# Seven-product block multiplication for the recurrent branch's projections, with gate projections set between the heads

## Chip, core and metric

The kernel runs on one NeuronCore of a Trainium2 chip. The metric is the device time of one execution in microseconds (us), the median over several runs. TensorE does the matrix products, VectorE (DVE), ScalarE (ACT) and GpSimd (POOL) the elementwise work, and SyncE (SP) issues nearly all DMAs. Each engine works through its own list of instructions in order; the lists are fixed when the program is built.

## The reference

One layer of a hybrid model on x of 1024 tokens by 1024 features, float32 throughout. All streams come from one projection of x:

```
(a_q ... b_u, b_v, b_z, c_q, c_k, c_v, c_if, c_o, c_z, m_g) = split(x @ w_in)
y_a = nsa(...) * silu(a_z)                       # sparse attention
y_b = spatial_gating(b_u, b_v, ...) * silu(b_z)  # 128x128 mixing per chunk of tokens
y_c = mlstm(c_q, c_k, c_v, c_if, c_o, ...) * silu(c_z)
merged = sum over 3 branches of sigmoid(m_g[branch]) * (y_branch @ w_br[branch])
r = ALPHA * x + merged @ w_out
out = layernorm(r + sigmoid(r @ ple_gate) * (p @ ple_w))
```

The recurrent branch `mlstm` has 4 heads of 128 features. For each head it passes c_q and c_k through a causal convolution of 4 taps, a bias and a silu; it then runs over 8 chunks of 128 tokens, with a state matrix carried from chunk to chunk; the result is normalized and multiplied by sigmoid(c_o) and silu(c_z). m_g holds 3 x 1024 gate features.

## The kernel before

**Number format.** Every product with x or another wide operand is made from split operands: each float32 tile is cut into a high part `hi` (a cast to the type that TensorE reads faster, by ACT) and a remainder `lo` (a subtraction on DVE), and hi x hi, lo x hi and hi x lo are summed in PSUM. So one 128x128x512 block product is three matmuls. A plain projection of 128 features (`wf`, then `proj_half` on L129 twice) takes 8 blocks of the 1024 inputs, 3 matmuls each, for two halves of 512 tokens: 48 matmuls. `load_w` (L92, L93) loads and splits its weights.

**Strassen for the gates.** The 24 blocks of gate features are taken in 12 pairs. A pair is a product of a 2x2 block matrix of weights (two feature blocks, two halves of the inputs) with a 2x2 block matrix of x (two halves of the inputs, two halves of the tokens). `strassen` (L886) makes it with seven block products instead of eight: 7 x 4 x 3 = 84 matmuls (L907). For each product the left operand is a sum of weight blocks (`total`, DVE, L899), split into `sh` (ACT, L893) and `sl` (DVE, L894); partial results are kept by ACT (L912), added by DVE (L945), and put through tanh by ACT (L947). The right operands are x's own tiles or the sums `T1` to `T4`, made once before the first pair (L861 to L884): DVE or POOL subtractions, then `split_op` (L857, L858).

**Order of the work.** The program is written with tile pools; a tool puts the instructions into each engine's list by its own estimate of when each is ready, taking the one that is first in program order among those ready, and adds the waits. When a pool is closed and another opened in its place, a tile of the new pool waits for those tiles of the old one that lay at the same addresses. Tiles of one tag share that tag's buffers.

The stages are: attention (fillers: a_z, b_u, b_z projections); then pool `pq`: the token-side value projections `proj_tok256` (L150) for b_v and then c_v (into `V1`, L686); the spatial gating (8 chunks c: L706, mixing matmuls L710 with `wT`, 4 DVE operations L713 and 4 L716 per chunk, one buffer `mt`); the four heads; then `pq` closes, `pg` opens, T1 to T4 and the 12 gate pairs; then `pf`, the merge of the branches (L956 on).

A head before: `conv_proj` twice (wf, taps L739 and L742, tanh and L745), the chunk loop (L766 to L804), small statistics (L805 to L814), the c_z and c_o projections into `oz` (L816 to L833), and transposes, product `yc` and store to `ysc` (L834 to L843). Each head has 4 plain projections.

Of the kernel before, what the change touches and what calls it, by code (L numbers as in the profile page):

```python
# [45 lines left out]
def hybrid_kernel(ctx, tc, xm, pT, wfm, wvg, wtm, cmpw1, cmpw2, cpos, vecs, sgwT, sgb,  # L46
# [680 lines left out]
    def conv_proj(i, nm):  # L727
        w = wf(FM["cq"] + i)
        xq = pq.tile([P, T + 4], F32, tag="xpad", bufs=1, name="xpad")
        nc.gpsimd.memset(xq[:, 0:4], 0.0)  # L730
        for half in range(2):
            po = pj()
            proj_half(po, w, half, xh, xl)
            nc.scalar.copy(xq[:, 4 + half * 512:516 + half * 512], po)
        r = pq.tile([P, T], F32, tag=nm, bufs=1, name=nm)

        def tap(j):
            return vec[:, C_CW + 4 * i + j:C_CW + 4 * i + j + 1]
        vv.tensor_scalar(out=r, in0=xq[:, 4:4 + T], scalar1=tap(3), scalar2=vec[:, C_CB + i:C_CB + i + 1],  # L739
                         op0=OP.mult, op1=OP.add)  # L740
        for j in range(3):
            stt(out=r, in0=xq[:, 1 + j:1 + j + T], scalar=tap(j), in1=r, op0=OP.mult, op1=OP.add)  # L742
        t = pq.tile([P, T], F32, tag="cth", bufs=1, name="cth")
        act(t, r, AF.Tanh, scale=0.5)
        stt(out=r, in0=t, scalar=1.0, in1=r, op0=OP.add, op1=OP.mult)  # L745
        return r

    for h in range(NH_C):
        yc = pq.tile([P, T], F32, tag="yc", bufs=4, name="yc")
        k2 = conv_proj(4 + h, "k2")  # L750
# [1 line left out]
        eb = pq.tile([P, NT, P], F32, tag="eb", bufs=1, name="eb")
        ub = pq.tile([P, NT, P], F32, tag="ub", bufs=1, name="ub")
        nc.sync.dma_start(ub.rearrange("p c t -> p (c t)"), uscr[0, h:h + 1, :].to_broadcast([P, T]))
        nc.sync.dma_start(eb.rearrange("p c t -> p (c t)"), uscr[1, h:h + 1, :].to_broadcast([P, T]))
        for c in range(NT):
            act(ub[:, c, :], ub[:, c, :], AF.Exp, bias=cols[:, 0, 8 * h + c:8 * h + c + 1], scale=-1.0)
        nc.gpsimd.affine_select(out=ub, in_=ub, pattern=[[0, NT], [1, P]], compare_op=OP.is_ge,
                                fill=0.0, base=0, channel_multiplier=-1)
        qe = pq.tile([P, T], F32, tag="qe", bufs=1, name="qe")  # L760
        for c in range(4):
            s = slice(c * 256, c * 256 + 256)
            nc.gpsimd.tensor_mul(qe[:, s], q2[:, s], eb.rearrange("p c t -> p (c t)")[:, s])
        nb = pq.tile([P, NT, 129], F32, tag="nb", bufs=1, name="nb")
        mv = pq.tile([P, NT, 2], F32, tag="mv", bufs=1, name="mv")
        C1 = None  # L766

        def intra(c):
            s = slice(c * P, c * P + P)
            psS = pst("st", 2, "ps_cs")  # L770
            mm(psS[:, 0:P], lhsT=k2[:, s], rhs=q2[:, s], start=True, stop=True)
            Wt = pq.tile([P, P], F32, tag="Wt", bufs=2, name="Wt")
            stt(out=Wt, in0=psS[:, 0:P], scalar=CS, in1=ub[:, c, :], op0=OP.mult, op1=OP.mult)
            ke = None
            if c < NT - 1:
                pk = pst("m", 2, "ps_k")
                nc.tensor.transpose(pk[:, 0:P], k2[:, s], ident)
                ke = pq.tile([P, P], F32, tag="ke", bufs=2, name="ke")
                nc.scalar.mul(ke, pk[:, 0:P], cols[:, 2, 8 * h + c:8 * h + c + 1])
            return Wt, ke  # L780

        nxt = intra(0)
        for c in range(NT):
            s = slice(c * P, c * P + P)
            Wt, ke = nxt
            if c < NT - 1:
                nxt = intra(c + 1)
            pn = pst("o", 2, "ps_n")
            mm(pn[:, 0:129], lhsT=Wt, rhs=V1[:, c, h, :], start=True, stop=(c == 0))
            if c > 0:  # L790
                mm(pn[:, 0:129], lhsT=qe[:, s], rhs=C1, start=False, stop=True)
            nc.scalar.copy(nb[:, c, :], pn[:, 0:129])
            s6 = pq.tile([P, 6], F32, tag="s6", bufs=2, name="s6")
            vv.bn_stats(out=s6, in_=nb[:, c, 0:P])
            vv.bn_aggr(out=mv[:, c, :], in_=s6)
            if c < NT - 1:
                pu = pst("m", 2, "ps_u")
                mm(pu[:, 0:129], lhsT=ke, rhs=V1[:, c, h, :], start=True, stop=True)
                Cn = pq.tile([P, 129], F32, tag="C1", bufs=2, name="C1")
                if C1 is None:  # L800
                    vv.tensor_copy(Cn, pu[:, 0:129])
                else:
                    stt(out=Cn, in0=C1, scalar=eb[:, c, P - 1:P], in1=pu[:, 0:129], op0=OP.mult, op1=OP.add)
                C1 = Cn  # L804
        dn = pq.tile([P, NT], F32, tag="dn", bufs=1, name="dn")  # L805
        stt(out=dn.unsqueeze(2), in0=nb[:, :, P:P + 1], scalar=-1.0, in1=nb[:, :, P:P + 1], op0=OP.mult, op1=OP.max)
        vv.tensor_max(dn, dn, cols[:, 1, 8 * h:8 * h + 8])
        vv.reciprocal(dn, dn)
        ve = pq.tile([P, NT], F32, tag="ve", bufs=1, name="ve")
        vv.tensor_mul(ve, mv[:, :, 1], dn)  # L810
        vv.tensor_mul(ve, ve, dn)
        vv.tensor_scalar_add(ve, ve, EPS)
        rs = rsqrt_small(pq, ve, [P, NT], "rsc")
        vv.tensor_mul(rs, rs, dn)  # L814

        oz = pq.tile([P, T], F32, tag="oz", bufs=1, name="oz")  # L816
        w = wf(FM["cz"] + h)
        for half in range(2):
            po = pj()
            proj_half(po, w, half, xh, xl)  # L820
            s = slice(half * 512, half * 512 + 512)
            act(oz[:, s], po, AF.Tanh, scale=0.5)
            stt(out=oz[:, s], in0=oz[:, s], scalar=1.0, in1=po, op0=OP.add, op1=OP.mult)
        w = wf(FM["co"] + h)
        for half in range(2):
            po = pj()
            proj_half(po, w, half, xh, xl)
            s = slice(half * 512, half * 512 + 512)
            t = tp.tile([P, 512], F32, tag="ge_a", bufs=2, name="oth")
            act(t, po, AF.Tanh, scale=0.5)  # L830
            stt(out=oz[:, s], in0=t, scalar=1.0, in1=oz[:, s], op0=OP.add, op1=OP.mult)
        vv.tensor_scalar(out=oz, in0=oz, scalar1=vec[:, C_NG + h:C_NG + h + 1], scalar2=0.25,
                         op0=OP.mult, op1=OP.mult)  # L833
        for hf in range(2):  # L834
            pt = pst("o", 2, "ps_h")
            for cc in range(4):
                c = 4 * hf + cc
# [371 lines left out]
```

## Time and profile before

| what | value |
|---|---|
| median of 3 runs | 1386.09 us (1385.65 to 1388.98) |
| profiled execution | 1386.04 us |
| its span, first to last instruction | 1384.3 us |
| mean granted TensorE clock | 0.994 of full |
| PE, PEld, DVE, ACT, POOL busy | 98%, 83%, 58%, 35%, 12% |

PE is TensorE's matmuls, PEld its weight loads, which run beside the matmuls. A matmul's bar in the profile is its duration; bars of neighbours overlap, so the time a matmul takes in a stream is read from one start to the next. L-numbers are lines of the kernel before. "x48" is a count. In a list of waits, "A <- B" says that A sat idle until B was done.

### The profile page before, as it was taken

The numbers are of one execution on the slowest core, as the hardware profiler recorded it, in microseconds if no ns is written. First come the engines' busy times: TensorE is split into PE (matmuls) and PEld (weight loads), VectorE is DVE, ScalarE is ACT, GpSimd is POOL, SyncE is SP. The second block draws the span as 40 slices with busy tenths as digits, with TensorE's granted clock in tenths as the row PEclk, the third lists the DMA queues.
The fourth block names the chain that finished last, engine by engine and source line by source line (L and its number), as shares of the span: only waits on it lengthen the run. The fifth ranks groups of instructions, "written<-read, shape, count | busy, mean of one in ns | idle before, by whom it ended". The sixth has DMA issues, their size and how long they took to land. (4 is left out here: it accounts for less than half of the span.)

```text
span 1384.3 us, 18935 instructions
## 1 busy us (share of the span) xinstructions
PE 1355.4 (98%) x7231; PEld 1148.0 (83%) x7231; DVE 804.4 (58%) x1882; ACT 484.9 (35%) x974; POOL 162.1 (12%) x179
## 2 busy tenths in 40 slices
PE   9999999999999999999999979999999999999997
PEld 7977888887888999988888868888888887888786
DVE  7236687536787636486755775544545545334855
ACT  6353424243343333122332354444442212223211
POOL 0011211101221110020100000000000344000312
PEclk9999999999999999999999989999999999999999
DMA  9131101111120032142113123232248543113211
GB/s 313 31 82 34 31 21 46 30 54 55 39 69 5 17 108 78 47 152 92 62 61 92 51 103 116 97 122 107 107 145 318 196 148 121 46 61 123 98 39 46
DMA packets 39420, 123.27 MB, mean 89 GB/s; under 512 B 4761, under 2 KB 7705, under 8 KB 39329
## 3 DMA queue, kind: packets, MB, share of 16 engines
q1 hardware_dynamic: 38368, 118.91, 25.1%
q0 software_dynamic: 960, 3.15, 1.0%
q8 instruction: 57, 0.93, 0.3%
q14 instruction: 35, 0.28, 0.1%
HBM read 98.91 MB, written 23.13 MB: 88 GB/s over the span
## 5 line engine op out<-in xcount | busy, mean ns | idle before, releaser
L129 PE MATMUL ps_pj<-xh,whi 128*128 128x512 f32 x544 | 217.3, 399 | 2.3 <-DVE QA L402 2.3
L129 PE MATMUL ps_pj<-xh,wlo 128*128 128x512 f32 x544 | 216.8, 399 | 0.0
L129 PE MATMUL ps_pj<-xl,whi 128*128 128x512 f32 x544 | 215.2, 396 | 0.0
L536 PEld LDWEIGHTS ps_o<-V,pt 128*128 128x128 f32 x912 | 117.5, 191 | 12.2 <-ACT pt L516 3.3
L129 PEld LDWEIGHTS ps_pj<-xh,whi 128*128 128x128 f32 x544 | 102.3, 188 | 22.8 <-PE ps_pj L129 3.9
L129 PEld LDWEIGHTS ps_pj<-xl,whi 128*128 128x128 f32 x544 | 102.4, 188 | 18.9
L129 PEld LDWEIGHTS ps_pj<-xh,wlo 128*128 128x128 f32 x544 | 102.7, 189 | 17.5
L536 PE MATMUL ps_o<-V,pt 128*128 128x65 f32 x912 | 116.6, 269 | 0.5 <-POOL pt L518 0.3
L92 ACT CAST whi<-wraw 128x1024 fp32r<-128x1024 f32 x62 | 65.0, 1048 | 106.8 <-PE ps_b L129 51.6
L516 ACT ACTIVATE pt<-ps_st 128x512 f32<-128x512 f32 x114 | 65.3, 594 | 103.9 <-PE ps_st L514 96.8
L93 DVE TENSOR_TENSOR wlo<-wraw,whi 128x1024 fp32r<-128x1024 f32 x62 | 81.2, 1310 | 20.5 <-ACT whi L92 20.3
L979 POOL TENSOR_TENSOR M<-M,gt 128x512 f32<-128x512 f32 x32 | 42.8, 1349 | 350.4 <-DVE gt L978 334.8
L129 PE MATMUL ps_b<-sp_hi,wlo 128*128 128x512 f32 x192 | 74.7, 389 | 0.0
L129 PE MATMUL ps_b<-sp_hi,whi 128*128 128x512 f32 x192 | 74.7, 389 | 0.0
L129 PE MATMUL ps_b<-sp_lo,whi 128*128 128x512 f32 x192 | 74.1, 390 | 0.0
L907 PE MATMUL ps_a<-op_hi,sh 128*128 128x512 f32 x144 | 56.0, 389 | 0.0
L907 PE MATMUL ps_a<-op_hi,sl 128*128 128x512 f32 x144 | 56.0, 389 | 0.0
L907 PE MATMUL ps_a<-op_lo,sh 128*128 128x512 f32 x144 | 56.0, 389 | 0.0
L894 DVE TENSOR_TENSOR sl<-ss,sh 128x512 fp32r<-128x512 f32 x48 | 33.1, 692 | 35.2 <-ACT sh L893 34.9
L1024 PE MATMUL ps_g<-gh,sp_hi 128*128 128x512 f32 (+1 forms) x144 | 52.7, 366 | 0.0
L1024 PE MATMUL ps_g<-gh,sp_lo 128*128 128x512 f32 (+1 forms) x144 | 52.7, 366 | 0.0
L1024 PE MATMUL ps_g<-gl,sp_hi 128*128 128x512 f32 (+1 forms) x144 | 52.6, 366 | 0.0
(360 smaller groups left out, 3117.7 us busy)
## 6 DMA issues: line engine op xcount, KB each, us to landing
wraw<-in_wfm_dram SPq DMA_DIRECT2D x34, 512.0 KB, 3.6
mraw<-in_wfm_dram SPq DMA_DIRECT2D x24, 512.0 KB, 3.6
gsc<-gt SPq DMA_DIRECT2D x24, 512.0 KB, 2.6
gt<-gsc SPq DMA_DIRECT2D x24, 512.0 KB, 6.0
xraw<-in_xm_dram SPq DMA_DIRECT2D x14, 512.0 KB, 6.8
wraw<-in_wbr_dram SPq DMA_DIRECT2D x12, 512.0 KB, 4.4
yraw<-ysc SPq DMA_DIRECT2D x12, 512.0 KB, 4.3
wraw<-in_wtm_dram SPq DMA_DIRECT2D x8, 512.0 KB, 3.8
```

Source lines behind the costliest of these rows:

```text
L92: nc.scalar.copy(hi[:, c], raw[:, c])
L93: vv.tensor_sub(lo[:, c], raw[:, c], hi[:, c])
L129: mm(po[:M, :], lhsT=a[:, k, :], rhs=b(k, half), start=(i == 0), stop=(i == n - 1))
L516: act(pt.rearrange("p h q -> p (h q)"), sp, AF.Exp)
L536: mm(po[:, h * 65:h * 65 + 65], lhsT=pt[:, h, :], rhs=V[:, j, vi, :], start=(first and h == 0), stop=last, skip_group_check=True)
L894: vv.tensor_sub(lo, src, hi)
L907: mm(bank, lhsT=l[a][:, k, :], rhs=r[b], start=first and k == 0 and i == 0, stop=k == K - 1 and i == 2, skip_group_check=True)
L979: nc.gpsimd.tensor_add(M[n][:, s], M[n][:, s], t[:, s])
L1024: mm(po[:, 0:n], lhsT=a[k][:, ts_], rhs=b[k][:, s], start=(k == 0 and i == 0), stop=(k == KT - 1 and i == 2))
```

## The change

- The eight plain projection pairs of the heads become Strassen pairs: c_k with c_q (`conv_pair`), c_z with c_o (`oz_pair`). All Strassen pairs share `strassen`; its product order becomes B11, T1, T2, B21, T3, B22, T4, its third bank comes from tag "st" instead of "o", and `sh`, `sl`, `ss` have 3 buffers instead of 4.
- T1 to T3 are made beside the b_v projections and T4 after the c_v projections, in a new pool `pt` that stays open below `pq` and `pg`.
- `pq` closes right after the spatial gating, and `pg` opens there. c_v is written to DRAM (`v1scr`) from small tiles `vs` and read back per head into a one-head `V1`.
- The 12 gate pairs are no longer one block: each head issues two of them (`mg_pair`), one between `conv_pair` and `oz_pair` and one after the head's chunks; four follow at the end. Their results `gt` use the weight tag "wlo" instead of "y".
- In the heads k2, q2, oz, eb, ub, qe, nb and the padded inputs take the shared tag "y" (8 buffers); the chunk's PSUM tiles move from "st" and "m" to "m" and "o". The first tap and the scaling of oz go from DVE to ACT; tanh of the convolution is made in halves.

```diff
+    right = {n: [None, None] for n in ("T1", "T2", "T3", "T4")}
+    t4 = []
+    for m in range(2):
+        b11, b12, b22, b21 = (yp.tile([P, T], F32, tag="y", bufs=YB, name="xraw") for _ in range(4))
+        for t, (mm_, j) in zip((b11, b12, b22, b21), ((m, 0), (m, 1), (m + 2, 1), (m + 2, 0))):
+            nc.sync.dma_start(t, xm[mm_, j])
+        vv.tensor_sub(b11, b12, b11)
+        right["T1"][m] = split_op(b11, pt_, "t", 12)
+        vv.tensor_sub(b12, b22, b12)
+        vv.tensor_sub(b22, b22, b11)
+        right["T2"][m] = split_op(b22, pt_, "t", 12)
+        right["T3"][m] = split_op(b12, pt_, "t", 12)
+        vv.tensor_sub(b21, b21, b22)
+        t4.append(b21)
...
-    V1 = pq.tile([P, NT, NH_C, 129], F32, name="V1")
+    v1scr = dr.tile([NH_C, P, NT, P], F32, name="v1scr")
     for wi in range(2):
         for i, po in enumerate(proj_tok256(wtm[2 + wi], xh, xl)):
...
+            vs = pq.tile([P, 2, 2, P], F32, tag="vs", bufs=2, name="vs")
+            nc.any.tensor_copy(out=vs.rearrange("p j a d -> p (j a d)"), in_=po)
+            for a in range(2):
+                nc.sync.dma_start(v1scr[2 * wi + a, :, 2 * i:2 * i + 2, :], vs[:, :, a, :])
+    for m in range(2):
+        right["T4"][m] = split_op(t4[m], xp, "x", 16)
...
+    pq_ctx.close()
+    pg_ctx = ExitStack()
+    pg_ = pg_ctx.enter_context(tc.tile_pool(name="pg", bufs=1))
+    pq = pg_
+    ng4 = pg_.tile([P, 4], F32, name="ng4")
...
+            hi = pg_.tile([P, 512], F32R, tag="sh", bufs=3, name="sh")[:, 0:w]
+            lo = pg_.tile([P, 512], F32R, tag="sl", bufs=3, name="sl")[:, 0:w]
...
+    def mg_pair(q):
+        gt = [wp.tile([P, T], F32, tag="wlo", bufs=WB, name="gt") for _ in range(2)]
...
+    def conv_pair(h):
...
+        strassen_fm(FM["ck"] + h, FM["cq"] + h, done)
...
+            act(r, x[:, 4:4 + T], AF.Identity, scale=tap(3), bias=vec[:, C_CB + i:C_CB + i + 1])
+            for j in range(3):
+                stt(out=r, in0=x[:, 1 + j:1 + j + T], scalar=tap(j), in1=r, op0=OP.mult, op1=OP.add)
+            for half in range(2):
...
+                stt(out=r[:, s], in0=t, scalar=1.0, in1=r[:, s], op0=OP.add, op1=OP.mult)
...
     for h in range(NH_C):
...
-        k2 = conv_proj(4 + h, "k2")
-        q2 = conv_proj(h, "q2")
+        k2, q2 = conv_pair(h)
+        mg_pair(2 * h)
+        oz = oz_pair(h)
+        V1 = pq.tile([P, NT, 129], F32, tag="V1", bufs=1, name="V1")
+        nc.gpsimd.memset(V1[:, :, 128:129], 1.0)
+        nc.sync.dma_start(V1[:, :, 0:P], v1scr[h])
...
+        nc.sync.dma_start(ysc[2][h], oz)
+        mg_pair(2 * h + 1)
+    for q in range(8, 12):
+        mg_pair(q)
     pg_ctx.close()
+    pt_ctx.close()
```

## Rows read from the trace of the kernel before

**Rows 1.** The page's first part: busy time, share of the span, instructions

```profile
PE 1355.4 (98%) x7231; PEld 1148.0 (83%) x7231; DVE 804.4 (58%) x1882; ACT 484.9 (35%) x974; POOL 162.1 (12%) x179
```

**Rows 2.** Waits of PE between 560 and 1060 us: total, times, longest

```profile
PE ps_a L907 <- ACT sh L893: 7.2, 1, 7.2
PE ps_n L791 <- POOL qe L763: 0.9, 1, 0.9
PE ps_b L907 <- ACT sh L893: 0.7, 1, 0.7
```

**Rows 3.** Windows: length, busy PE, PEld, DVE, ACT, POOL, PEclk, DMA share, GB/s

```profile
400.00:425.00 25.00, 24.95 (x149) 20.96 (x149) 20.34 (x63) 8.71 (x21) 4.68 (x6) 1.00 0.09 28
...
495.00:529.00 34.00, 33.56 (x278) 33.17 (x277) 17.25 (x38) 13.19 (x21) 3.15 (x3) 1.00 0.39 127
...
529.00:575.00 46.00, 46.00 (x385) 46.00 (x384) 18.32 (x46) 12.93 (x28) 1.09 (x1) 1.00 0.21 69
...
577.00:594.30 17.30, 17.30 (x106) 15.27 (x105) 16.50 (x66) 0.82 (x2) 0.00 (x0) 1.00 0.12 37
...
600.00:625.00 25.00, 24.10 (x137) 19.92 (x136) 19.20 (x41) 8.77 (x21) 8.31 (x7) 1.00 0.34 123
...
636.80:689.60 52.80, 52.80 (x271) 44.24 (x269) 32.99 (x81) 17.19 (x39) 4.09 (x7) 1.00 0.22 70
...
797.00:802.00 5.00, 0.00 (x0) 0.00 (x0) 2.16 (x4) 1.22 (x2) 0.00 (x0) 0.53 0.52 211
...
805.00:808.00 3.00, 3.00 (x10) 2.33 (x9) 3.00 (x4) 2.17 (x3) 0.00 (x0) 0.57 0.00 0
808.00:811.00 3.00, 3.00 (x15) 2.48 (x14) 2.39 (x3) 1.54 (x2) 0.00 (x0) 1.00 0.00 0
...
850.00:1000.00 150.00, 150.00 (x664) 124.20 (x663) 75.88 (x110) 64.89 (x112) 0.00 (x0) 1.00 0.32 113
```

**Rows 4.** Timeline of PE: two projection matmuls, 51 starts apart: start, duration

```profile
699.66 0.39 PE L129 MATMUL ps_pj<-xl,whi 128*128 128x512 f32 x1
...
711.22 0.40 PE L129 MATMUL ps_pj<-xl,whi 128*128 128x512 f32 x1
```

**Rows 5.** Timeline around the closing of pool pq, 794 to 808 us

```profile
793.96 0.40 PE L129 MATMUL ps_pj<-xl,whi 128*128 128x512 f32 x1
794.19 1.04 PE L840 MATMUL ps_h<-ident,nb 128*128 128x128 f32 x8
...
797.93 0.33 SPq L843 DMA_DIRECT2D ysc<-yc  x1
800.71 0.69 DVE L899 TENSOR_TENSOR ss<-mraw 128x512 f32<-128x512 f32 x1 [2.81 <-issue]
800.78 1.05 ACT L857 CAST op_hi<-xraw 128x1024 fp32r<-128x1024 f32 x1 [5.79 <-DMA ysc<-yc]
...
802.40 0.79 PE L907 MATMUL ps_a<-xh,sh 128*128 128x512 f32 x1 [7.17 <-ACT sh L893]
...
807.75 0.40 PE L907 MATMUL ps_a<-xh,sh 128*128 128x512 f32 x1
```

**Rows 6.** Timeline of the spatial gating: its first and last instructions

```profile
574.74 0.28 PE L150 MATMUL ps_st<-whi,xl 128*128 128x256 f32 x1
...
574.86 1.02 PE L691 MATMUL ps_m<-wT,ones 128*128 128x512 f32 x2
...
575.73 1.05 PE L710 MATMUL ps_m<-wT,vb 128*128 128x128 f32 x8
...
575.93 1.13 DVE L694 SCALAR_TENSOR_TENSOR bt<-ps_m,vec,bsb 128x128 f32<-128x128 f32 x4
576.53 0.48 PE L129 MATMUL ps_pj<-xh,whi 128*128 128x512 f32 x1
...
576.97 1.21 DVE L93 TENSOR_TENSOR wlo<-wraw,whi 128x1024 fp32r<-128x1024 f32 x1
...
593.86 0.48 DVE L716 SCALAR_TENSOR_TENSOR yb<-mt,yb 128x128 f32<-128x128 f32 x2
```

**Rows 7.** DVE groups in one Strassen stretch, 850 to 1000 us

```profile
L894 DVE TENSOR_TENSOR sl<-ss,sh 128x512 fp32r<-128x512 f32 x31 | 21.5, 693 | 23.2 <-ACT sh L893 22.9
```

**Rows 8.** Costliest DVE groups of two heads, 636.8 to 742.3 us

```profile
L93 DVE TENSOR_TENSOR wlo<-wraw,whi 128x1024 fp32r<-128x1024 f32 x8 | 9.8, 1221 | 0.0
L742 DVE SCALAR_TENSOR_TENSOR k<-xpad,vec,k 128x1024 f32<-128x1024 f32 x6 | 7.7, 1283 | 0.2
```

**Rows 9.** Timeline at the end of the gate pairs, SP, DVE and PE

```profile
1033.02 2.28 SPq L951 DMA_DIRECT2D gsc<-gt  x2
...
1025.39 1.23 DVE L93 TENSOR_TENSOR wlo<-wraw,whi 128x1024 fp32r<-128x1024 f32 x1
...
1034.16 0.39 PE L129 MATMUL ps_b<-sp_hi,whi 128*128 128x512 f32 x1
1034.38 0.39 PE L129 MATMUL ps_b<-sp_hi,wlo 128*128 128x512 f32 x1
```

**Rows 10.** DMA issues: count, KB each, median us to landing

```profile
gsc<-gt SPq DMA_DIRECT2D x24, 512.0 KB, 2.6
...
ysc<-yc SPq DMA_DIRECT2D x4, 512.0 KB, 4.0
```

More of the change, by code (lines that the diff above doesn't have):

```diff
@@ L26 @@
 YB = 8
+YW = 1032
 WARM = 8
@@ L569, in fill_az @@
             else:
-                z = tp.tile([P, 512], F32, tag="zz", bufs=1, name="zz")
+                z = pa2.tile([P, 512], F32, tag="zz", bufs=1, name="zz")
                 silu2(z, po, 512)
@@ L618, in hybrid_kernel @@
         nc.sync.dma_start(ysc[0][i], ya[i])
+    pt_ctx = ExitStack()
+    pt_ = pt_ctx.enter_context(tc.tile_pool(name="pt", bufs=1))
+    cols = pt_.tile([P, 3, 32], F32, name="cols")
     pq_ctx = ExitStack()
@@ L632, in hybrid_kernel, with split_op @@
             gelu2(vb[i][:, :, wi * 256:wi * 256 + 256], po.rearrange("p (t n) -> p t n", t=2), 512)
+    def split_op(src, pl_, tg, bf):
+        hi = pl_.tile([P, T], F32R, tag=tg, bufs=bf, name="op_hi")
+        lo = pl_.tile([P, T], F32R, tag=tg, bufs=bf, name="op_lo")
+        nc.scalar.copy(hi, src)
+        vv.tensor_sub(lo, src, hi)
+        return hi, lo
+    right = {n: [None, None] for n in ("T1", "T2", "T3", "T4")}
[12 more added lines that the diff above has]
+        t4.append(b21)
+    for n, m, j in (("B11", 0, 0), ("B21", 2, 0), ("B22", 2, 1)):
+        right[n] = [(xhs[m + r][j], xls[m + r][j]) for r in range(2)]
     gi = pq.tile([32, P], F32, name="gi")
@@ L725, in hybrid_kernel @@
         nc.sync.dma_start(ysc[1][i], yb[i])
[L727 to L746, printed above, removed]
@@ L748, in hybrid_kernel @@
-    for h in range(NH_C):
-        yc = pq.tile([P, T], F32, tag="yc", bufs=4, name="yc")
-        k2 = conv_proj(4 + h, "k2")
-        q2 = conv_proj(h, "q2")
[L752 to L837, printed above, removed]
-                vv.tensor_scalar(out=nb[:, c, 0:P], in0=nb[:, c, 0:P], scalar1=mv[:, c, 0:1],
-                                 scalar2=rs[:, c:c + 1], op0=OP.subtract, op1=OP.mult)
-                nc.tensor.transpose(pt[:, cc * P:cc * P + P], nb[:, c, 0:P], ident)
-            s = slice(hf * 512, hf * 512 + 512)
-            vv.tensor_mul(yc[:, s], pt, oz[:, s])
-        nc.sync.dma_start(ysc[2][h], yc)
@@ L883, in hybrid_kernel @@
-    for n, m, j in (("B11", 0, 0), ("B21", 2, 0), ("B22", 2, 1)):
-        right[n] = [(xhs[m + r][j], xls[m + r][j]) for r in range(2)]
+    pq = pg_
+    ng4 = pg_.tile([P, 4], F32, name="ng4")
+    vv.tensor_scalar_mul(ng4, vec[:, C_NG:C_NG + 4], 0.25)
     def strassen(raw0, raw1, K, right, done):
@@ L924, in strassen, with strassen_fm @@
         c2 = kept(a)
+        c = pst("st", 2, "ps_c")
+        product(c, a12, "B21", True)
+        done(0, 0, c, c1)
+        product(a, total(a11, a21, OP.subtract), "T3", False)
+        done(1, 1, a, c5)
         product(b, total(a12, s2, OP.subtract), "B22", False)
         done(0, 1, b, c2)
-        product(a, total(a11, a21, OP.subtract), "T3", False)
-        done(1, 1, a, c5)
-        c = pst("o", 2, "ps_c")
-        product(c, a12, "B21", True)
-        done(0, 0, c, c1)
         product(a, a22, "T4", False)
         done(1, 0, a, None)
-    WTAGS = (("wraw", 2), ("whi", WB), ("wlo", WB))
-    for q in range(12):
-        tg, bf = WTAGS[q % 3]
-        raw = [wp.tile([P, 1024], F32, tag=tg, bufs=bf, name="mraw") for _ in range(2)]
-        for i in range(2):
-            nc.sync.dma_start(raw[i], wfm[FM["mg"] + 2 * q + i])
-        gt = [yp.tile([P, T], F32, tag="y", bufs=YB, name="gt") for _ in range(2)]
+    rawn = [0]
+    def strassen_fm(f0, f1, done):
+        tg = ("wraw", "whi")[rawn[0] % 2]
+        rawn[0] += 1
+        raw = [wp.tile([P, 1024], F32, tag=tg, bufs=2, name="mraw") for _ in range(2)]
+        for t, f in zip(raw, (f0, f1)):
+            nc.sync.dma_start(t, wfm[f])
+        strassen(raw[0], raw[1], 4, right, done)
+    def mg_pair(q):
+        gt = [wp.tile([P, T], F32, tag="wlo", bufs=WB, name="gt") for _ in range(2)]
         def done(i, j, bank, kept):
@@ L947, in done, with tap @@
             act(gt[i][:, j * 512:j * 512 + 512], bank, AF.Tanh, scale=0.5)
-        strassen(raw[0], raw[1], 4, right, done)
+        strassen_fm(FM["mg"] + 2 * q, FM["mg"] + 2 * q + 1, done)
         for i in range(2):
             nc.sync.dma_start(gsc[2 * q + i], gt[i])
+    def conv_pair(h):
+        xq = [yp.tile([P, YW], F32, tag="y", bufs=YB, name="xpad") for _ in range(2)]
+        for t in xq:
+            nc.gpsimd.memset(t[:, 0:4], 0.0)
+        def done(i, j, bank, kept):
+            dst = xq[i][:, 4 + j * 512:516 + j * 512]
+            if kept is None:
+                nc.scalar.copy(dst, bank)
+            else:
+                vv.tensor_add(dst, bank, kept)
+        strassen_fm(FM["ck"] + h, FM["cq"] + h, done)
+        res = []
+        for x, i, nm in ((xq[0], 4 + h, "k2"), (xq[1], h, "q2")):
+            r = yp.tile([P, T], F32, tag="y", bufs=YB, name=nm)
+            def tap(j):
+                return vec[:, C_CW + 4 * i + j:C_CW + 4 * i + j + 1]
+            act(r, x[:, 4:4 + T], AF.Identity, scale=tap(3), bias=vec[:, C_CB + i:C_CB + i + 1])
+            for j in range(3):
+                stt(out=r, in0=x[:, 1 + j:1 + j + T], scalar=tap(j), in1=r, op0=OP.mult, op1=OP.add)
+            for half in range(2):
+                s = slice(half * 512, half * 512 + 512)
+                t = tp.tile([P, 512], F32, tag="ge_a", bufs=2, name="cth")
+                act(t, r[:, s], AF.Tanh, scale=0.5)
+                stt(out=r[:, s], in0=t, scalar=1.0, in1=r[:, s], op0=OP.add, op1=OP.mult)
+            res.append(r)
+        return res
@@ new lines, in oz_pair, with done @@
+    def oz_pair(h):
+        oz = yp.tile([P, T], F32, tag="y", bufs=YB, name="oz")
+        def done(i, j, bank, kept):
+            o = oz[:, j * 512:j * 512 + 512]
+            if kept is not None:
+                vv.tensor_add(kept, bank, kept)
+                bank = kept
+            first = (i, j) in ((0, 0), (1, 1))
+            if first and i == 1:
+                act(o, bank, AF.Tanh, scale=0.5)
+                return
+            t = o if first else tp.tile([P, 512], F32, tag="ge_a", bufs=2, name="oth")
+            act(t, bank, AF.Tanh, scale=0.5)
+            if i == 0:
+                stt(out=t, in0=t, scalar=1.0, in1=bank, op0=OP.add, op1=OP.mult)
+            if not first:
+                a, b = (o, t) if i == 0 else (t, o)
+                stt(out=o, in0=a, scalar=1.0, in1=b, op0=OP.add, op1=OP.mult)
+        strassen_fm(FM["cz"] + h, FM["co"] + h, done)
+        nc.scalar.mul(oz, oz, ng4[:, h:h + 1])
+        return oz
```

114 lines of the change are left out of this document (74 added, 40 removed).

## Prediction, made before the changed kernel was run

> **What bounds the kernel now.** I read the page's busy times first, then PE's waits, then windows by stage, then the timeline where PE stops. PE is busy for 1355 of 1384.3 us [rows 1], and between 560 and 1060 us, where the change lies, it waits only 8.8 us in all, 7.2 of them at one place [rows 2]. In the heads (636.8 to 689.6 us) and in the gate pairs (850 to 1000 us) it has no idle time at all, while DVE is at 62% and 51% [rows 3]. So the stretch to be changed costs the number of its matmuls times their spacing, plus what is lost at the seams between pools. The spacing is not the bar: the bars say 0.39, but 51 starts take 711.22 - 699.66 = 11.56 us, 0.2267 us each [rows 4]. By the bars, a matmul removed would look worth 1.7 times what it is.
>
> The 7.2 us lie at the seam from `pq` to `pg`. The last projection matmul starts at 793.96, eight transposes follow, then PE stands still until 802.40 [rows 5]: new tiles lie where the last head's `yc` was, and ACT waits for its store (5.8 us). Then the clock is low: the granted clock was 0.53 between 797 and 802 and 0.57 between 805 and 808, about half, that is the 1.2 GHz level, and 1.00 from 808 on [rows 3].
>
> **A, fewer matmuls.** Each head had 4 projections of 48 matmuls, 192; two Strassen pairs have 2 x 84 = 168. Four heads save 96. At 0.2267 us [rows 4] that is 21.8 us off, all on PE's path.
>
> **B, the old seam goes.** From 793.96 to 807.75 is 13.8 us [rows 5]. The work in it is 11 matmuls of 0.2267 and a group of eight small ones at 0.80 (575.73 to 576.53 [rows 6]), 3.3 us. So 10.5 us are lost there now. In the new order the T sums are made long before, and the heads' last stores overlap with gate pairs: 10.5 us off.
>
> **C, the new seam.** `pq` now closes right behind the spatial gating, and the first `sh`, `sl`, `ss` lie where `wT`, `ones`, `mt` and `vb` lay (I added up the tiles' sizes in order of first use). Before, PE filled the gating with the first convolution projection, whose weights and outputs were in other pools: it is busy for all of 577 to 594.3, with DVE at 16.5 of 17.3 us [rows 3]. After, everything PE could fill with needs `sh`. The gating is DVE's: from 575.93 to 594.34 [rows 6], 18.4 us, with one weight split of 1.2 us in it [rows 6] that goes, and two T4 remainders of the same size (1.22 us [rows 8]) that come: 19.6 us. It starts 1.07 us behind the last c_v product [rows 6], and the first `sl` takes 0.69 us more [rows 7]: Strassen runs 21.4 us behind it. PE's own work in that time is 0.87 us for the bias sums and 8 mixing groups of 0.80 [rows 6], 7.3 us. So 14.1 us are lost. At best, if the mixing is spread among the c_v products, some 2 us (the last chunk's DVE work) would be left; at worst 3 us more, if T work is left over.
>
> **D, the clock at the new seam.** Not shown before in this shape. From one side nothing: in the window 600 to 625 PE had a gap of 0.9 us and the clock stayed at 1.00 [rows 2, 3]. From the other, the old restart: 10 matmuls from 802.40 to 807.75 took 5.35 us where 2.27 would do [rows 5], 3.1 us. The gaps here are some 1.3 us between groups, eight times, and lie between the two rows; I take 1.5.
>
> The Trainium skill ("TensorE: Matmul & The Clock Gate", section "A second HAM failure mode: psum-queue depth-cycling") speaks against this seam: a TensorE that is idle briefly but often between groups of matmuls swings between its clock levels and loses throughput each time. The window with one short gap doesn't show it; by the rule D would be 3.9 (below).
>
> **E, the start of the branch merge.** Now the weights' remainder for the merge is ready at 1026.6, long before PE needs it at 1034.38 [rows 9]. After, it goes into a "wlo" buffer which holds the last pair's `gt` until that is stored. The store is issued at 1033.02 [rows 9] and lands 2.6 us later [rows 10], then 1.23 us of DVE: 1036.9, 2.5 us late, of which PE can fill some 0.5 with other products of the high part. I take 2.0; ends 0 (another buffer is free) and 3.5 (DVE is in another operation of 1.2).
>
> **F, DVE in the heads.** A gate pair is 84 x 0.2267 = 19.0 us of PE and, at 75.9 of 150 us [rows 3], 9.6 us of DVE. A head's DVE work was 33.0 us per 52.8 [rows 3]; without four weight splits of 1.22 [rows 8] and with four Strassen pairs it is at most 33.0 - 4.9 + 38.5 = 66.6 us. Its PE time is 52.8 - 192 x 0.2267 + 4 x 19.0 = 85.4 us. So DVE is at 78%. The nearest row is attention at 400 to 425 us: DVE 81%, PE 24.95 of 25 [rows 3], which speaks for 0.2 us per head; but left operands are now only two products ahead, and a convolution's taps (1.28 us each [rows 8]) come first in program order. I take 1 us per head, 4 in all; ends -0.9 (the present wait for `qe` goes [rows 2]) and 20 (below).
>
> **Costed at nothing.** T1 to T3 beside b_v: 14 DVE operations of 1.22 us [rows 8], 17 us, under stretches where DVE had 17.25 of 34 and 18.3 of 46 us [rows 3]; without that cover the c_v weights come late, some 1.2 us each. The c_v round trip: it is loaded while the `oz` pair's 19 us of products run, against 4.0 us for a store of that size [rows 10]. The V1 load waits on SP for the previous head's last chunk, and behind it stand the next pairs' weights and `gt` stores; they are a pair ahead, so PE would feel a hold above some 15 us. The V1 memset goes to POOL, ahead of the mask and `qe`, which need the same head anyway. ACT gets casts and copies, but was at 35% [rows 1].
>
> **Sum,** against the profiled execution (1386.04, at the median of 1386.09): -21.8 - 10.5 + 14.1 + 1.5 + 2.0 + 4.0 = -10.7, so 1375.3 us.
>
> **Rivals.**
> 1. *DVE holds up the heads (slower).* k2 and q2 together need six taps of 1.28 and 2.8 us of silu, 10.4 us, all ahead of the gate pair's left operands in program order. With two products prepared (24 x 0.2267 = 5.4 us), PE would stand 5 us per head, 20 in all: 1375.3 + 16 = 1391. It turns the sign once a head loses more than (10.7 + 4)/4 = 3.7 us. For it: 78% and the smaller buffers. Against it: attention at 81% [rows 3], and dependent taps leave openings (a weight split gets in between head operations even now). Chance 0.20.
> 2. *The new seam is filled.* The gating's statistics are ready early, since DVE is idle for 27.7 of the 46 us of the c_v products [rows 3]; if the mixing groups are put among those, C is 2 and D 0: 1375.3 - 14.1 - 1.5 + 2 = 1361.7. Against it: the ones product L691, which needs nothing of c_v, stands right behind the last c_v matmul [rows 6], so PE's list goes by program order. Chance 0.15.
> 3. *PE's clock is low through the whole new seam.* Mixing groups of 1.6 us still fit under some 2 us of DVE per chunk, the last one adds 0.8, and the restart costs 3.1 instead of 1.5: 1375.3 + 2.4 = 1377.7. For it: the fall at 797 [rows 3]. Against it: there PE had stood still for 7 us. It is what the Trainium skill's section named under D would give. Chance 0.12.
>
> That the change saves no matmuls is excluded by the count.
>
> **How the numbers follow.** My forecast, with seam exposed and heads nearly undisturbed, has 0.53; its own range, from the ends of D and E and of F up to 10, is 1368 to 1382. A measurement of this kernel can tell about 0.3%, 4.2 us: faster is below 1381.9, slower above 1390.2. Faster: 0.50 of the forecast's, all of rival 2, 0.10 of rival 3, 0.75. Rival 1 goes half to no change and half to slower: slower 0.10, same 0.15. The range reaches from just below rival 2 to just short of rival 1's full price: 1360 to 1390.
>
> **What would show it.** Right: some 7135 matmuls; no long wait of PE after the last head; a stretch of some 20 us behind the last c_v product in which only L710-like groups run on PE and DVE is full; a PE wait of 2 us at the first merge product; DVE near 78% in the heads with PE above 98%. Wrong: PE idle many times in each head, waiting for `sh` or `sl` (rival 1); mixing groups among the c_v products (rival 2); a clock near 0.5 between them (rival 3).

## The result, and the profile after

The changed kernel takes 1394.63 us (median of 4 runs, 1394.37 to 1397.22) against 1386.95 us for the kernel before on the same chip (4 runs, 1385.65 to 1388.98): a ratio of 1.0058, interval 1.0040 to 1.0076. It is slower by more than the 0.3% that such a measurement can tell, where 1375.3 us and faster were forecast, with a range of 1360 to 1390. The profiled execution has a span of 1392.6 us, 8.3 more than before. L-numbers below are lines of the changed kernel: Strassen's matmuls are L786 (L907 before), the token-side projections L151 (L150), the mixing L741 (L710), `sh` L772, `sl` L773.

The first part of the page after, which answers to [rows 1]:

```profile
PE 1355.7 (97%) x7135; PEld 1134.0 (81%) x7135; DVE 849.4 (61%) x1974; ACT 521.9 (37%) x1040; POOL 158.0 (11%) x181
```

There are 7231 - 7135 = 96 matmuls fewer, as counted, and yet PE is busy as long as before. So the loss has two parts: the matmuls that are left take longer, and PE has 8 us more without work. The second part is in the waits of PE between 480 and 1080 us (total, times, longest; compare [rows 2]):

```profile
PE ps_m L741 <- DVE mt L744: 4.9, 6, 0.9
PE ps_m L706 <- ACT bc L701: 4.6, 1, 4.6
PE ps_a L786 <- ACT sh L772: 4.2, 1, 4.2
PE ps_h L970 <- DVE nb L968: 1.7, 4, 0.4
PE ps_b L130 <- DVE wlo L94: 1.3, 1, 1.3
```

The 7.2 us of [rows 2] at the old seam are gone. The first and third lines are the new seam. The second lies in the middle of the c_v projections, where PE was full before ([rows 3], 529 to 575).

The first part, longer matmuls, shows in the timeline of PE among the last gate pairs: two rows, 45 starts apart.

```profile
977.92 0.40 PE L786 MATMUL ps_b<-xl,sh 128*128 128x512 f32 x1
...
988.42 0.40 PE L786 MATMUL ps_a<-op_lo,sh 128*128 128x512 f32 x1
```

That is 10.50 us for 45, 0.2333 each, where the kernel before had 0.2267 [rows 4]. Its own gate pairs had 0.2267 too, 10.20 us for 45:

```profile
899.97 0.39 PE L907 MATMUL ps_a<-op_lo,sh 128*128 128x512 f32 x1
...
910.17 0.39 PE L907 MATMUL ps_b<-xl,sh 128*128 128x512 f32 x1
```

The bars differ by some 0.01 us only, so a view of bars would hide it. There are now 1680 Strassen matmuls (20 pairs x 84): 1680 x 0.0066 = 11.1 us.

The new seam, timeline of PE (start, duration) with the cast that releases it:

```profile
581.35 0.28 PE L151 MATMUL ps_st<-whi,xl 128*128 128x256 f32 x1
581.47 1.02 PE L722 MATMUL ps_m<-wT,ones 128*128 128x512 f32 x2
582.33 1.05 PE L741 MATMUL ps_m<-wT,vb 128*128 128x128 f32 x8
...
593.53 1.16 PE L741 MATMUL ps_m<-wT,vb 128*128 128x128 f32 x8 [0.89 <-DVE mt L744]
595.58 1.16 PE L741 MATMUL ps_m<-wT,vb 128*128 128x128 f32 x8 [0.89 <-DVE mt L744]
...
600.25 0.62 ACT L772 CAST sh<-mraw 128x512 fp32r<-128x512 f32 x1 [17.95 <-DVE yb L747]
...
600.92 0.80 PE L786 MATMUL ps_a<-xh,sh 128*128 128x512 f32 x1 [4.18 <-ACT sh L772]
...
605.61 0.39 PE L786 MATMUL ps_b<-op_hi,sh 128*128 128x512 f32 x1
```

Each mixing group now waits for DVE, 2.05 us from one to the next, and the first Strassen cast waits for the gating's last operation. From 581.47 to 605.61 is 24.1 us with 0.87 + 8 x 0.80 + 12 x 0.2333 = 10.1 us of work in it: 14.0 lost.

Windows after (columns as in [rows 3]): the half-clock stretch in c_v, the mixing, the half-clock stretch behind it, a piece of the heads, a piece of the later stretch.

```profile
546.50:553.30 6.80, 5.05 (x22) 4.71 (x23) 3.44 (x11) 1.95 (x5) 0.00 (x0) 0.50 0.41 121
581.50:597.60 16.10, 9.96 (x68) 7.98 (x66) 14.28 (x59) 0.58 (x1) 0.00 (x0) 1.00 0.19 49
597.70:604.50 6.80, 3.58 (x8) 2.57 (x9) 6.49 (x18) 1.85 (x3) 0.13 (x1) 0.50 0.72 277
...
640.00:760.00 120.00, 119.56 (x559) 95.63 (x558) 83.11 (x170) 58.92 (x120) 9.96 (x14) 1.00 0.29 97
900.00:1030.00 130.00, 129.58 (x586) 103.85 (x585) 78.40 (x156) 61.70 (x116) 4.38 (x5) 1.00 0.42 142
```

In these windows the clock falls to 0.50, the 1.2 GHz level, during the two stops of PE (4.6 and 4.2 us) and stays there past them; between the mixing groups of this run it stays at 1.00. In the heads PE is busy 99.6% of the time with DVE at 69%.

The stop in the c_v projections, by the timeline of DVE, SP, ACT and PE:

```profile
531.56 0.40 DVE L679 TENSOR_TENSOR_SCAN cm<-gi 32x128 f32<-32x128 f32 x1
...
533.77 0.33 SPq L684 DMA_DIRECT2D lscr<-lastv  x1
538.37 0.27 SPq L686 DMA_DIRECT2D lrow<-lscr  x1
541.38 0.24 SPq L691 DMA_DIRECT2D mscr<-mrow  x1
542.48 0.31 SPq L693 DMA_DIRECT2D mp<-mscr  x1
...
546.81 0.27 DVE L694 TENSOR_SCALAR cm<-cm,mp 32x128 f32<-32x128 f32 x1
...
547.89 0.30 ACT L701 ACTIVATE bc<-bc 32x128 f32<-32x128 f32 x1
...
548.25 0.31 PE L706 MATMUL ps_m<-ident,bc 32*128 32x32 f32 x1 [4.58 <-ACT bc L701]
```

This is the scan over the recurrent gates: a chain of small DVE operations and two DRAM round trips. In the kernel before, the same scan ran at 512.72:

```profile
512.72 0.41 DVE L649 TENSOR_TENSOR_SCAN cm<-gi 32x128 f32<-32x128 f32 x1
```

Now it runs at 531.56, behind the T1 to T3 work that stands ahead of it in program order and waits for its own loads (3.1 and 2.0 us of DVE's time). PE's three transposes of the result keep their place in PE's list, and PE stands there until 548.25.

### The profile page after: what moved, and what is told of

The parts are those of the page before. It is cut to its first block, busy times and chain, and to the rows that moved or that the text cites. A ratio compares the mean times of both kernels' runs of the same rounds, so it can differ in the third digit from the quotient of the medians.

```text
span 1392.6 us, 18947 instructions
## 1 busy us (share of the span) xinstructions
PE 1355.7 (97%) x7135; PEld 1134.0 (81%) x7135; DVE 849.4 (61%) x1974; ACT 521.9 (37%) x1040; POOL 158.0 (11%) x181
## 4 chain that ended last, share of the span: by engine, by line
PE 85%; DVE 6%; DMA 3%; ACT 3%; issue 2%; POOL 0%; SPq 0%; DVEq 0%; ACTq 0%; POOLq 0%
PE ps_pj L130 18%; PE ps_a L786 15%; PE ps_b L130 9%; PE ps_b L786 8%; PE ps_o L537 7%; PE ps_g L1050 5%; PE ps_c L786 4%; PE ps_st L514 2%; PE ps_pj L151 2%; PE ps_v L139 2%; PE ps_st L515 2%; PE ps_e L1090 2%; PE ps_st L151 1%; PE ps_s L493 1%; DMA xraw<-in_xm_dram 1%
## 5 line engine op out<-in xcount | busy, mean ns | idle before, releaser
L130 PE MATMUL ps_pj<-xh,whi 128*128 128x512 f32 x288 | 115.5, 401 | 2.3 <-DVE QA L403 2.3
L130 PE MATMUL ps_pj<-xh,wlo 128*128 128x512 f32 x288 | 114.8, 398 | 0.0
L130 PE MATMUL ps_pj<-xl,whi 128*128 128x512 f32 x288 | 114.5, 398 | 0.0
L786 PE MATMUL ps_a<-op_hi,sl 128*128 128x512 f32 x240 | 95.2, 397 | 0.0
L786 PE MATMUL ps_a<-op_lo,sh 128*128 128x512 f32 x240 | 95.2, 396 | 0.0
L786 PE MATMUL ps_a<-op_hi,sh 128*128 128x512 f32 x240 | 94.7, 395 | 0.0
L773 DVE TENSOR_TENSOR sl<-ss,sh 128x512 fp32r<-128x512 f32 x80 | 54.8, 689 | 61.8 <-ACT sh L772 58.6
L772 ACT CAST sh<-mraw 128x512 fp32r<-128x512 f32 x60 | 37.3, 622 | 82.6 <-PE ps_c L786 33.6
L130 PEld LDWEIGHTS ps_pj<-xh,whi 128*128 128x128 f32 x288 | 54.2, 188 | 13.6 <-PE ps_pj L130 3.9
L130 PEld LDWEIGHTS ps_pj<-xl,whi 128*128 128x128 f32 x288 | 54.2, 188 | 9.8
L130 PEld LDWEIGHTS ps_pj<-xh,wlo 128*128 128x128 f32 x288 | 54.3, 189 | 9.0
L772 ACT CAST sh<-ss 128x512 fp32r<-128x512 f32 x80 | 49.6, 620 | 26.0 <-PE ps_b L786 25.3
L786 PEld LDWEIGHTS ps_a<-op_hi,sl 128*128 128x128 f32 x240 | 45.2, 188 | 11.0
```

Source lines behind the costliest of these rows:

```text
L130: mm(po[:M, :], lhsT=a[:, k, :], rhs=b(k, half), start=(i == 0), stop=(i == n - 1))
L772: nc.scalar.copy(hi, src)
L773: vv.tensor_sub(lo, src, hi)
L786: mm(bank, lhsT=l[a][:, k, :], rhs=r[b], start=first and k == 0 and i == 0, stop=k == K - 1 and i == 2, skip_group_check=True)
```

## The experiments

The theory after the result: three separate losses, (1) the place of the Strassen operands in SBUF, (2) the late scan, (3) the open seam. Rivals: DVE in the heads is the cause (the prediction's rival 1), or Strassen's new product order and banks are what makes its matmuls slow.

Below, "less" is against the changed kernel's 1394.63 us. The sets of runs were on different chips, on which the kernel before had medians of 1385.88 to 1386.95 us, so such a difference is good to about 1 us.

**a_pad: the place of `sh` and `sl`.** By the tiles' sizes in order of first use, `ng4` (16 bytes, taking 32) puts `sh`, `sl` and `ss` 32 bytes past where they would be.

```diff
-    ng4 = pg_.tile([P, 4], F32, name="ng4")
+    ng4 = pg_.tile([P, 32], F32, name="ng4")[:, 0:4]
```

> The changed kernel with the tile ng4 padded from 16 bytes to 128 bytes per partition, so that sh, sl, ss and cp behind it in pool pg begin at a multiple of 128 bytes instead of 32 bytes past one. Theory 1 (placement of the left operands): in the changed kernel the Strassen matmuls start 0.2333 us apart where those of the kernel before started 0.2267 apart, because sh and sl lie 32 bytes off; here they come back to 0.2267, and 1680 x 0.0066 = 11 us go: about 1383. Rival (the rows of x, the banks or the other engines' traffic slow them): the spacing stays at 0.2333 and the time within 2 us of 1394.6.

1389.19 us (1386.11 to 1390.33), ratio to before 1.0022 (1.0011 to 1.0032), 5.4 us less than the changed kernel. From start to start, products with x's own tiles are back at 0.227; those with T1 to T3 stay at 0.229 to 0.238. Three rows of PE's timeline, 12 and 24 starts apart (B11 with x's own tiles, then T1 and T2):

```profile
1016.26 0.39 PE L786 MATMUL ps_a<-xh,sh 128*128 128x512 f32 x1
...
1018.98 0.40 PE L786 MATMUL ps_b<-op_hi,sh 128*128 128x512 f32 x1
...
1024.57 0.39 PE L786 MATMUL ps_c<-xh,sh 128*128 128x512 f32 x1
```

The twelve with x's tiles take 0.2267 each, the 24 with T1 and T2 0.2329. The moving operands of these, the T tiles, still lie behind `cols` (3 x 32 floats, 384 bytes), while `sh` and `sl` now lie behind 384 + 128 = 512 bytes. So the new order and banks are not the cause, and both kinds of operand count. Only four of the seven products were mended (960 matmuls, 6.3 us by the count), so that 5.4 us came and not the 11 expected.

**a_scan: the scan ahead of T1 to T3.**

```diff
-    right = {n: [None, None] for n in ("T1", "T2", "T3", "T4")}
...
     vv.tensor_scalar_mul(cols[:, 2, :], pc_[:, 64:96], CS)
+    right = {n: [None, None] for n in ("T1", "T2", "T3", "T4")}
...
     v1scr = dr.tile([NH_C, P, NT, P], F32, name="v1scr")
```

> The changed kernel with the T1 to T3 block moved behind the gate scan in program order. Theory: PE's wait of 4.6 us at the three transposes of the scan (L706), and the half clock for 6.8 us after it, come from DVE doing T work ahead of the scan; here the scan is done by the time the transposes come, as in the kernel before: 4.6 + about 2.5 = 7 us less, about 1387.5. Rival (the scan is late because of its DRAM round trips behind other loads on SP): the wait stays, within 2 us of 1394.6.

1388.66 us (1387.1 to 1391.81), ratio 1.0023 (1.0013 to 1.0032): 6.0 us less. PE's wait at the transposes is gone, and the clock is 1.00 over 500 to 585 us. Right behind that, in the middle of the mixing, the granted clock fell to 0.50 for 3.4 us, which it had not done in the changed kernel. The group there (timeline of PE), and the window:

```profile
585.42 3.82 PE L739 MATMUL ps_m<-wT,vb 128*128 128x128 f32 x16 [0.88 <-DVE mt L742]
```

```profile
585.40:588.80 3.40, 3.38 (x14) 3.11 (x15) 3.17 (x14) 0.00 (x0) 0.00 (x0) 0.50 0.00 0
```

**a_fill: the second c_v projection behind the gating in program order.**

```diff
-    for wi in range(2):
+    def cv_proj(wi):
...
+    cv_proj(0)
...
         nc.sync.dma_start(ysc[1][i], yb[i])
+    cv_proj(1)
+    for m in range(2):
+        right["T4"][m] = split_op(t4[m], xp, "x", 16)
     pq_ctx.close()
```

> The changed kernel with the second c_v projection and the T4 sums put behind the spatial gating in program order, still ahead of the closing of pq. Theory: some 14 us are lost at the new seam because nothing is left that PE could do beside the gating; with 23 us of products there the mixing groups no longer stand alone, the seam costs 2 to 4 us, and the time falls by 10 to 12 us, to about 1383. Rival (the seam's loss is the wait for the first left operands, whatever PE does before): the wait of 4 us and the half clock stay, and less than 6 us are gained.

1389.59 us (1387.7 to 1392.96), ratio 1.0028 (1.0018 to 1.0037): 5.0 us less, not the 10 to 12 expected: the rival's case. The mixing is hidden now, but PE's waits between 520 and 620 us are

```profile
PE ps_a L788 <- ACT sh L774: 5.7, 1, 5.7
PE ps_m L706 <- ACT bc L701: 4.8, 1, 4.8
```

and ACT's between 585 and 600 us say why:

```profile
ACT sh L774 <- DMA v1scr<-vs: 4.3, 1, 4.3
```

The first `sh` lies where the last `vs` was, and waits for that tile's store to DRAM. It is the old seam again ([rows 5], where ACT waited 5.8 us for the store of `yc`).

**a_fill2: as a_fill, with `vs` in a tag of another pool.**

```diff
-            vs = pq.tile([P, 2, 2, P], F32, tag="vs", bufs=2, name="vs")
+            vs = tp.tile([P, 512], F32, tag="ge_a", bufs=2, name="vs").rearrange("p (j a d) -> p j a d", j=2, a=2)
```

> The changed kernel with the second c_v projection and T4 behind the spatial gating in program order, as in a_fill, and the small tiles vs moved from pool pq to the shared tag ge_a. Theory: in a_fill the mixing groups were hidden, and what was left of the seam (5.7 us of wait and a restart at half clock) was the store of the last vs, whose place pool pg takes over; without that tile in pq the first left operands are ready before the c_v products end, and the seam costs under 1.5 us: 1394.6 - 14 = 1381. Rival (the seam is the closing of the pool as such): the wait stays and the time is 1388 to 1390.

1381.74 us (1379.69 to 1383.06), ratio 0.9966 (0.9953 to 0.9978): 12.9 us less than the changed kernel, and the only PE wait left in that stretch is the scan's 4.6 us. So the seam cost some 13 us. The pool closes in this run too, so the closing as such is not the cost. It is what last used the places that the next pool's first tiles take: the gating's last operation in the changed kernel, the store of `vs` in a_fill.

**a_512: all Strassen operands at multiples of 512 bytes.**

```diff
-    cols = pt_.tile([P, 3, 32], F32, name="cols")
+    cols = pt_.tile([P, 4, 32], F32, name="cols")[:, 0:3, :]
...
-    ng4 = pg_.tile([P, 4], F32, name="ng4")
+    ng4 = pg_.tile([P, 128], F32, name="ng4")[:, 0:4]
```

> The changed kernel with two tiles made larger and nothing else: cols (384 bytes per partition) to 512, ng4 to 512, so that the T tiles and sh, sl, ss, cp all begin at multiples of 512 bytes from the base of pool pt, as they did from the base of pool pg in the kernel before. Theory 1: with sh and sl at a good place the products with x's own tiles went back to 0.227, those with the T tiles (384 bytes off) did not; now all 1680 come to 0.2267 us: 11 us less than the changed kernel, about 1383.5, and 5 to 6 less than with ng4 alone padded. Rival (traffic of the other engines in the heads slows the products with T tiles): those stay at 0.229 to 0.238 us and the time at about 1389.

1385.39 us (1384.14 to 1386.74), ratio 0.9997 (0.9988 to 1.0006): 9.2 us less, where 11 were expected. All Strassen matmuls are at 0.227 again.

**b_skew, b_skew128, b_skew256, b_skew512: the place alone, in the kernel before.** An unused tile ahead of `sh`; nothing else is changed.

```diff
+    skew = pg_.tile([P, 8], F32, name="skew")
+    vv.memset(skew, 0.0)
+
     def strassen(raw0, raw1, K, right, done):
```

Here of 32 bytes; the others have 32, 64 and 128 floats.

> The kernel before with a tile of 32 bytes per partition put into pool pg ahead of sh, sl, ss and cp, and nothing else (the T tiles stay where they were). Theory 1 (placement of the left operands): its 1008 Strassen matmuls go from 0.2267 to 0.2333 us, 6.7 us slower, about 1393. Rival: no change, 1386 to 1388.

> The kernel before with a tile of 128 bytes per partition ahead of sh, sl, ss and cp in pool pg. If a left operand at any place that is not a multiple of 512 bytes slows the matmul, the Strassen matmuls start 0.232 to 0.235 us apart; if a multiple of 128 bytes is enough, 0.2267.

> As b_skew512, with 256 bytes. If half of 512 is enough, 0.227 us from start to start and about 1386 us; if it takes a multiple of 512, some 0.232 or more and 1391 to 1395 us.

> The kernel before with a tile of 512 bytes (per partition) ahead of the Strassen operands, set once by DVE. If the place modulo 512 bytes is what counts, the Strassen matmuls start 0.227 us apart as in the kernel before (the 32-byte tile gave 0.232 to 0.235, the 128-byte one 0.229 to 0.238) and the time is that of the kernel before within 0.2%. If any shift of these tiles, or the added tile with its memset, is the cost, it is some 6 us slower, as with 32 and 128 bytes.

| tile | time, us | ratio to before | mean from start to start, about 995 of the 1008 matmuls |
|---|---|---|---|
| 32 bytes | 1392.19 | 1.0047 (1.0032 to 1.0062) | 0.2333 |
| 128 bytes | 1394.2 (one run) | | 0.2333 |
| 256 bytes | 1385.97 (one run) | | 0.2267 |
| 512 bytes | 1386.35 | 1.0000 (0.9991 to 1.0010) | 0.2267 |

Timeline of PE with 32 bytes, rows 45 starts apart (10.51 us):

```profile
977.88 0.40 PE L910 MATMUL ps_c<-xl,sh 128*128 128x512 f32 x1
...
988.39 0.40 PE L910 MATMUL ps_a<-op_lo,sh 128*128 128x512 f32 x1
```

and with 512 bytes (10.20 us):

```profile
977.92 0.39 PE L910 MATMUL ps_a<-xh,sl 128*128 128x512 f32 x1
...
988.12 0.39 PE L910 MATMUL ps_b<-xh,sl 128*128 128x512 f32 x1
```

The kernel before loses 1008 x 0.0066 = 6.7 us to a tile of 32 bytes (measured 6.3 more), and nothing to one of 512. The added tile and its memset are thus no cost; the place is. A shift of 256 is harmless and one of 128 is not.

**a_best: a_512, a_scan and a_fill2 together.**

> All three repairs together: places at multiples of 512 bytes (11 us), T1 to T3 behind the gate scan in program order (6 us), the gating beside the second c_v projection with vs in tag ge_a (13 to 14 us). If the three losses are independent: 1394.6 - 31 = 1363 to 1366, faster than the kernel before by 1.5%. If DVE is the bound behind them: over 1372.

1365.4 us (1365.03 to 1365.65), ratio 0.9853 (0.9838 to 0.9868), faster than both kernels. The three gains alone add up to 9.2 + 6.0 + 12.9 = 28.1 us, and together they give 29.2: within the uncertainty, the losses are independent. PE's waits left behind 480 us include

```profile
PE ps_h L970 <- DVE nb L968: 2.2, 4, 0.6
...
PE ps_b L130 <- DVE wlo L94: 1.4, 1, 1.4
PE ps_m L687 <- ACT bc L682: 1.0, 1, 1.0
```

and the whole stretch from the first Strassen pair on is one window at full clock:

```profile
592.00:1010.00 418.00, 415.58 (x1938) 339.80 (x1937) 290.00 (x574) 205.89 (x385) 19.73 (x29) 1.00 0.32 109
```

**a_block: a_best with the gate pairs in one block behind the heads.** What the interleaving alone is worth.

```diff
-        mg_pair(2 * h)
...
-        mg_pair(2 * h + 1)
-    for q in range(8, 12):
+    for q in range(12):
         mg_pair(q)
```

> The best version so far (1365.4 us) with the twelve gate pairs in one block behind the heads, as in the kernel before; all else kept. If the interleaving of the gate pairs is what makes the switches between Strassen products and the chunk's small matmuls dear (some 10 us), and DVE has room, it is faster, down to 1356. If the gate pairs are what gives DVE time in the heads, the heads become DVE's: by the prediction's figures a head has 66.6 - 2 x 9.6 = 47.4 us of DVE against 85.4 - 2 x 19.0 = 47.4 us of PE, so at best 95% of DVE's time is full while PE waits: 3 to 8 us lost per head, 1377 to 1397 us, with PE waiting for DVE or ACT many times between 592 and 790 us. If neither, 1365 within 0.3%.

1372.28 us (1371.16 to 1372.83): 6.9 us more than a_best. PE's waits between 590 and 1040 us, and a window of the heads:

```profile
PE ps_k L925 <- DVE Wt L921: 4.9, 4, 1.3
PE ps_h L969 <- DVE nb L967: 2.2, 4, 0.6
```

```profile
592.00:720.00 128.00, 124.50 (x602) 101.11 (x602) 111.04 (x236) 67.61 (x132) 12.80 (x16) 1.00 0.26 84
```

DVE is at 111.04 of 128 us, 87%, and PE waits 4.9 us for the chunk's masked weights, against 0.2 in a_best. So the interleaved gate pairs do give DVE time, and the direction of the DVE theory was right, at a price below its 3 to 8 us per head. The other theory failed: without the interleaving it isn't faster.

**a_y: a_best with all tiles of tag y at 4096 bytes.**

```diff
-        xq = [yp.tile([P, YW], F32, tag="y", bufs=YB, name="xpad") for _ in range(2)]
...
+        xq = [yp.tile([P, T], F32, tag="y", bufs=YB, name="xpad") for _ in range(2)]
...
-                stt(out=r, in0=x[:, 1 + j:1 + j + T], scalar=tap(j), in1=r, op0=OP.mult, op1=OP.add)
+                stt(out=r[:, 3 - j:T], in0=x[:, 0:T - 3 + j], scalar=tap(j), in1=r[:, 3 - j:T], op0=OP.mult, op1=OP.add)
...
-        nb = yp.tile([P, NT, 129], F32, tag="y", bufs=YB, name="nb")
+        nb = yp.tile([P, NT, P], F32, tag="y", bufs=YB, name="nb")
+        nd = pq.tile([P, 64], F32, tag="nd", bufs=1, name="nd")[:, 0:NT]
...
-            nc.scalar.copy(nb[:, c, :], pn[:, 0:129])
+            nc.scalar.copy(nb[:, c, :], pn[:, 0:P])
+            nc.scalar.copy(nd[:, c:c + 1], pn[:, P:P + 1])
```

> The best version so far (1365.4 us) with the tiles of tag y at 4096 bytes each, as in the kernel before, instead of 4128: the convolution's inputs lose their four zero columns (each tap is added from its own column on), and nb loses its 129th column, which goes to a small tile with one more ACT copy per chunk. In the best version a step from a 128x512 matmul to one of the chunk's small ones takes 363 ns on average and from small to small 138 ns; in the kernel before 264 and 125 ns. If the place of k2, q2, qe and nb is the cause, these fall back, 60 x 0.1 + 240 x 0.013 = 9 us, of which 2.4 are waits: some 1358 us; the 56 matmuls of the last stage that read y tiles go back from 0.233 to 0.227 too, 0.4 us. If the cause is what the products in between wait for (fresh operands, the shared banks), the steps stay and the time is 1365 within 0.3%. The 32 added ACT copies of 8 x less than 1 us per head lie beside PE, and could cost up to 2 us where the product after next waits for the bank.

1367.81 us (1366.47 to 1369.5), no faster than a_best. The steps stay: 379 ns on average from a 128x512 matmul to a small one (60 times), 139 from small to small (240 times). The place of these tiles is not what makes the steps long.

## Why the prediction was wrong, point by point

**A, fewer matmuls: the count right, the spacing wrong.** 96 fewer came, worth -21.8. The step that failed is that all matmuls left would keep the 0.2267 us of [rows 4]. By the tiles' sizes, the T tiles came to lie 384 bytes, `sh` and `sl` 416 bytes past a multiple of 512 counted from the base of pool `pt`, and 1680 matmuls took 0.2333: +11.1 by the count, 9.2 by a_512. The sum had no term for it, and no range for the spacing. This is the largest error; without it (a_512, 1385.39) the time would have been within the range, though still 10 us above the forecast.

**B, the old seam: right.** No stop behind the last head.

**C and D, the new seam: right.** 15.6 us were forecast, 14.0 measured. PE stood for 19.45 - 7.3 = 12.2 us before the first Strassen product at 600.92 (C: 14.1), and the first 12 products took 4.69 us instead of 2.80 (D: 1.9 against 1.5). The gating was a little shorter than its bound, as T4's remainders did not lie in it.

**Costed at nothing, T1 to T3 beside b_v: wrong.** The prediction weighed DVE's free time there and named the late c_v weights as what would suffer. This is the second step that failed: it did not ask which chain with a deadline stands behind the T work in DVE's list: the gate scan, whose end PE needs in the middle of c_v. It ran 531.56 - 512.72 = 18.8 us later, PE stood 4.6 us, and the half clock took 2.5 more (5.05 us of PE's busy time in the window from 546.50). Measured by a_scan: 6.0.

**E, the merge's start: right,** 1.3 against 2.0, and by the mechanism named: DVE waited 3.5 us for the store of the last `gt` before it could write the `wlo` tile.

**F, the heads: mechanism absent, size too small.** DVE did not hold up PE for `sh` or `sl`; nowhere in the heads is there a wait of this kind, and DVE was at 69% in the piece shown, not 78%. But the steps between Strassen's products and the chunk's small matmuls cost more. I worked this out from the starts of all matmuls in the heads: before (600 to 794 us) a step from a 128x512 matmul to a small one took 264 ns on average (50 times) and one from small to small 125 (243 times); after, 341 (60 times) and 138 (240 times). With the small steps back (49 of 34 ns, now 60 of 41) that is 56.0 against 45.1 us; 10 steps more at 0.227 are 2.3 of it, and 8.6 are a loss, of which 1.7 are listed as waits. In a_best it is 10.1. The forecast was 4. Such a step took either 226 to 237 ns or over 300: 17 of 49 were long before, 40 of 60 after. The cause is not settled: a_block has the same long steps (median 318 ns, before 235) without the interleaving, and a_y with other places. That the chunk's PSUM tiles now lie in tags "m" and "o" was not tried alone.

**The sum.** -21.8 - 10.5 + 11.1 + 4.6 + 2.5 + 14.0 + 1.3 + 8.6 = +9.8, against +8.3 in the spans. Of this the forecast lacked the spacing (11.1), the late scan (4.6 + 2.5) and 4.6 in the heads; the seam and the merge came 1.6 and 0.7 cheaper than forecast. The forecast's own range was also added up wrongly: its ends give 1366.9 to 1384.4, not 1368 to 1382. The measurement lies above either. And from a_best, which has the first three losses taken away: 1386.04 - 21.8 - 10.5 + 1.4 + 10.1 = 1365.2, measured 1365.4.

**The rivals.** Rival 1 gave the right sign for a reason that did not come. Rival 2 was not what this program did: the ones product still stands right behind the last c_v matmul, as argued. Made by hand (a_fill2) a filled seam gives 12.9 us, against the 13.6 priced. Rival 3 did not come in this run: the clock was 1.00 over all of the mixing, with a stop of 0.9 us in nearly every group, and it fell only during the stops of 4.6 and 4.2 us. But it came in part where the same gating ran in a_scan and a_512: there the granted clock fell to 0.50 for 3.4 us in the middle of the mixing (from 585.4 and from 591.6 us), with no stop above 0.9 us before it. The fall by itself cost nothing, as the rival had it, since the groups still fit under DVE's time: from the ones product to the first Strassen product a_scan took 596.88 - 577.47 = 19.4 us, as long as the changed kernel. The first 12 products behind it took longer, 5.58 us in a_scan and 5.13 in a_512 against 4.69. The rule of the Trainium skill named under D ("TensorE: Matmul & The Clock Gate", section "A second HAM failure mode: psum-queue depth-cycling") thus agrees with those two traces; in those of the changed kernel and of a_pad the clock stayed at 1.00 through the same groups. Why it fell in two of the four is not shown.

## What to carry to other kernels

Price a matmul from start to start, and when a change opens a pool or puts a small tile ahead of matmul operands, work out where the operands will lie: here two small tiles (16 and 384 bytes) cost 9.2 us, near half of the 21.8 that 96 fewer matmuls saved. When work is moved beside an engine with free time, look for the chain with a deadline that stands behind it in program order, rather than for the engine's share. And where a pool closes and another opens in its place, the new pool's first tiles wait for the last use of whatever lay there, a store to DRAM as well as an operation; see to it that this use is long over.
